# Output projection of the mixer in written order, with the low halves of five activation blocks formed between its blocks

## The chip, the core and the metric

The kernel runs on one core of a Trainium2 chip. A core has five engines with instruction queues of their own: TensorE (PE; its weight loads are shown as PEld), VectorE (DVE), ScalarE (ACT), GpSimd (POOL) and SyncE (SP), which here only issues DMA transfers. The metric is the device time of one execution in microseconds, as the median of several runs. Beside the timed runs stands one execution that the hardware profiler recorded; all rows of a profile are of that execution, and its times are counted from the start of its span.

## The reference, cut to what matters

One layer of a streaming encoder over 512 tokens of 1024 features, in float32:

```python
ada = silu(c) @ w_ada + b_ada
sh1, sc1, g1, sh2, sc2, g2 = split(ada, 6)
h = modulate(rmsnorm(x, norm1_g), sh1, sc1)
z = h @ w_in                                   # five parts of 512 columns
y_a = gate_b * causal_dwconv(gate_c * xa, conv_a_w)
y_b = rg_lru(causal_dwconv(xr, conv_b_w) + conv_b_b, ...) * gelu(gr)
y = concat([head_rmsnorm(y_a), head_rmsnorm(y_b)]) @ w_out     # the output projection
x = x + g1 * y
h = modulate(rmsnorm(x, norm2_g), sh2, sc2)
q = h @ w_q                                    # 8 heads, two halves of 64
# per token and head: the best 16 of 128 keys in each half, the best 16 of their sums,
# softmax g over them, and expert numbers idx
act = gelu(expert_u[idx] . h);  coef = g * act
x = x + g2 * sum(coef * expert_v[idx])
out = rmsnorm(x, final_g)
```

There are 16384 experts. `act` and the sum over `expert_v` are what takes most of the time.

## The kernel before

**Split products.** Most products of float32 matrices are made of three matmuls in a faster type (float32r). A weight block of 1024 x 128 is loaded raw, its high half is the rounded copy that ACT writes (`high`, L74), its low half the difference that DVE writes (`low`, L79); `split_w` does both. `mm3` then issues, for each of the eight slices of 128, high weight by high input (L88), high weight by low input (L89) and low weight by high input (L90). The ring buffers `wraw`, `whi` and `wlo` have four tiles each, and a load into a ring waits until the tile four places earlier has been read.

**Stages, in order.** (1) Norm of x, the first adaLN columns, and the input projection: 20 blocks of `w_in`, between them convolutions, the recurrence and the norm of each head (`head_norm`, L487 to L504), which writes the eight parts of y as halves `ybuf_h` and `ybuf_l`. (2) The output projection: eight blocks of `w_out`, each followed by the residual update of one part of x (`xs`, L618, on DVE) and by the sum of squares (`sq_sum`: square L219 on ACT, addition L221 on DVE). The parts of y are taken in the order 4, 0, 5, 1, 6, 2, 7, 3, in which the head norms deliver them. (3) The second norm: the last update (L628), the mean square of each token (`stat`, L204, and L635), the transposes of x that are stored for the end (`x1_mm`, L588, and `x1_out`, L594, L595), and the modulated h in halves. (4) The query projection, eight blocks of `w_q`, the scores, and the first searches. (5) The activation stage: 124 blocks of 128 experts against 320 tokens that are treated densely; the product with all experts is made on PE, while DVE does the searches, the gate matrices and, for the other 192 tokens' part, dot products with gathered rows of `expert_u`. (6) The value stage: 128 blocks of `expert_v` (and the last four activation blocks), with three matmuls for each product (L1345), while DVE sums gathered rows for 128 tokens (L1083). (7) The final norm.

**Unsplit blocks.** In the activation stage, block 0 is formed in the query stage. Blocks 1 to 11 (`k < FN`, `FN = 12`) are not split: PE multiplies the raw float32 weights by the float32 input `h2f` (L1159), eight matmuls instead of 24. From block 12 on they are split: `w_high(k + 3)` and `w_low(k + 2)` run some blocks ahead. Blocks 5 to 11 are loaded straight into the rings `wlo` and `whi`, which are not needed for halves then.

**The adaLN pieces.** The columns of the second gate (`g2`) come from `ada_gate2`: eight pieces of `w_ada` of 128 x 1024 are loaded on SP (L129), scaled by the conditioning (L159) and added up on DVE (L163, 128 x 1024 each); a pair of matmuls with a column of ones sums over partitions into a row (`row_mm`, L138), ACT copies the row (L143), PE transposes it (four, L146), DVE adds the bias (L150), and the columns are stored to DRAM (`g2d`, L194). Before, this is the last part of the generator `ada_it`, which is stepped between the blocks of the mixer.

**What sets the order.** A planner orders the instructions of each engine by dependences and estimated costs, except inside a `manual_schedule` region: there, each engine issues the region's instructions in the order in which they are written. Where a region's instructions fall among those outside it, and the order across engines, stay with the planner. Before, such a region begins at block 7 of the output projection and ends in the second norm (at part 2 of h); another holds the activation and value stages. In the activation stage the written order itself is made by a small plan: `pe`, `dve` and `ac` add up estimated costs, and for each block DVE is given further work (searches, gates, dot products) as long as `dve[0] < RHO * pe[0]`.

Of the kernel before, what the change touches and what calls it, by code (L numbers as in the profile page):

```python
# [8 lines left out]
F32 = mybir.dt.float32  # L9
# [8 lines left out]
T = 512  # L18
D = 1024
KB = 8  # L20
# [14 lines left out]
def block_kernel(ctx, tc, xT, small, w_ada1, w_ada, b_ada, w_in, w_r, w_i, w_out, w_q, keys, uT, u, v, final_g, out):  # L35
# [46 lines left out]
    def split_w(raw):  # L82
        hi = high(raw)
        return hi, low(raw, hi)
# [47 lines left out]
    def ada_rows():  # L132
        pr = psA.tile([128, T], F32, name="ps_row")
        nc.vector.memset(pr, 0.0)
        return pr
# [19 lines left out]
    def ada_sum(q, every):  # L155
        acc = first.get(q)
        if acc is None:
            acc = piece(0, q, "wacc", 2)
        nc.vector.tensor_scalar(acc, acc, cl[:, 0:1], None, op0=OP.mult)  # L159
        for k in range(1, KB):  # L160
            if k % every == 0:
                yield
            nc.vector.scalar_tensor_tensor(acc, piece(k, q), cl[:, k:k + 1], acc, op0=OP.mult, op1=OP.add)  # L163
        return acc
# [21 lines left out]
        yield  # L186

    def ada_gate2():
        acc = yield from ada_sum(3, 1)
        pr = ada_rows()  # L190
        for b in range(2):
            row_mm(pr, b, ones, acc, True, True)
        ada_cols(pr, 40, 8)
        nc.sync.dma_start(g2d.rearrange("b (m p) -> p (b m)", p=128), adac[:, 40:48])  # L194
        yield
# [258 lines left out]
    def ada_rest():  # L454
        norm2 = ada_norm2()
        for i in range(19):
            if i % 2 == 0:
                next(gate1, None)
            next(norm2, None)
            yield  # L460
        yield from ada_gate2()
    ada_it = ada_rest()


# [129 lines left out]
        nc.scalar.activation(xn, pt, AF.Copy)  # L594
        nc.gpsimd.dma_start(x1d[t * 128:(t + 1) * 128, e * 512:(e + 1) * 512], xn)  # L595

    osp = {}
    qraw, qsp = {}, {}
    for m in range(KB):
        if m + 2 < KB:  # L600
            oraw[m + 2] = load_w(w_out[m + 2])
        else:
            qraw[m + 2 - KB] = load_w(w_q[m + 2 - KB])
        if m < KB - 1:
            osp[m] = split_w(oraw[m])
        if m >= KB - 2:
            for _ in ada_it:
                pass
            osp[KB - 1] = osp.get(KB - 1) or split_w(oraw[KB - 1])
        if m == KB - 1:  # L610
            norm2 = ExitStack()
            norm2.enter_context(tc.manual_schedule())
        hi, lo = osp.pop(m)
        ps = psZ.tile([128, T], F32, name="ps_z", bufs=3)
        mm3(ps, hi, lo, lambda k: ybuf_h[:, k, :], lambda k: ybuf_l[:, k, :], kord, True, True)
        if m == KB - 1:
            break
        nc.vector.scalar_tensor_tensor(xs[:, m, :], ps, adac[:, 16 + m:17 + m], xs[:, m, :], op0=OP.mult, op1=OP.add)  # L618
        sq_sum(m, True)
        next(ada_it, None)  # L620
    mx.close()
    adx.close()
    qp = pro.enter_context(tc.tile_pool(name="qp", bufs=2))
# [476 lines left out]
    def w_load(k):  # L1100
        if k < len(jobs):
            kind, i = jobs[k]
            if 5 <= k < FN:
                raw = wring.tile([128, KB, 128], FR, name=("wlo", "whi")[k % 2], bufs=WB).bitcast(F32)
                nc.sync.dma_start(raw, uT[i])
                wraw[k] = raw
                return
            if k >= K5 and (k - K5) % 5 == 4:
                wraw[k] = gp.tile([128, KB, 128], F32, name="raw5")
                nc.sync.dma_start(wraw[k], uT[i] if kind == "u" else  # L1110
                                  v[vorder[i] * 128:(vorder[i] + 1) * 128, :].rearrange("p (k e) -> p k e", k=KB))
                return
            wraw[k] = load_w(uT[i] if kind == "u" else
                             v[vorder[i] * 128:(vorder[i] + 1) * 128, :].rearrange("p (k e) -> p k e", k=KB))

    def w_high(k):
        if FN <= k < len(jobs):
            whi[k] = high(wraw[k])

    def w_low(k):  # L1120
        if FN <= k < len(jobs):
            wlo[k] = low(wraw.pop(k), whi[k])
            settle()

# [6 lines left out]

    def weights(k):
        w_ahead(k)
        w_low(k + 2)

    act = {0: act0}
# [15 lines left out]
    def u_chunk(k, pool):  # L1152
        c = jobs[k][1]
        if c:
            ps = pool.tile([128, NU], F32, name="ps_act", bufs=3 if pool is psE else 2)
            if k < FN:
                raw = wraw.pop(k)
                for j in range(KB):
                    nc.tensor.matmul(ps, raw[:, j, :], h2f[j // 2][:, j % 2], start=j == 0, stop=j == KB - 1)  # L1159
            else:  # L1160
                mm3(ps, whi.pop(k), wlo.pop(k), hd, ld, range(KB), True, True)
            u_evict()
            unread.append((c, ps))
        q = c // 2 - 2
        if c % 2 == 0 and 0 <= q < v0 // 2:
            spill(q)
        pe[0] += FPE if c and k < FN else 3530
        dve[0] += 0 if c and k < FN - 2 else 1140
        ac[0] += 450 if c and k < FN - 3 else 1400

    gbuf, g16, gdone = {}, {}, set()
    coef = {}
# [95 lines left out]
        w_load(k)  # L1268
    for k in range(1, 3):
        w_high(k)  # L1270
    w_low(1)
    manual = ExitStack()
    manual.enter_context(tc.manual_schedule())
# [169 lines left out]
GS = 32768.0  # L1443
AB = 3
GPE = 460
FN = 12
DX = 0.3
FPE = 4400
SE = 0.65
# [71 lines left out]
```

## Time and profile before

| | us |
|---|---|
| median of 3 runs | 1329.12 (1328.17 to 1332.12) |
| profiled execution | 1328.57 |
| its span, first to last instruction | 1326.8 |
| TensorE busy | 1304.6 (98%) |
| VectorE busy | 1215.5 (92%) |
| ScalarE busy | 728.2 (55%) |
| GpSimd busy | 503.8 (38%) |

In a row of the timeline stand the start, the duration, the engine, the line of the kernel, the operation, what is written and read with the shapes, and in brackets the idle time of the engine just before and what ended it. A group of instructions by line shows the count, then busy time, mean duration in ns, and the idle time before with what ended it. A matmul's record is longer than its distance to the next one, because matmuls overlap; the distance of two starts is what one costs. In this execution the output projection's matmuls run from 159.9 to 207.1 us, the activation stage's unsplit blocks from 279.4 to 326.7, and the value stage's matmuls from 770.9 on.

### The profile page before, as it was taken

Reading aid. Unit: us, or ns where it says so; the run is one execution under the profiler, and the core shown is the slowest. Engines: PE = TensorE matmul, PEld = TensorE weight load, DVE = VectorE, ACT = ScalarE, POOL = GpSimd, SP = SyncE. Lnnn points to the kernel's source line nnn. Section 1 sums busy time; section 2 is a strip of 40 time slices with the busy share of each in tenths; the row PEclk is TensorE's granted clock in tenths of the full one; section 3 lists DMA queues with packets and bytes.
Section 4 is the critical chain, followed back from the end, with each engine's and each line's share of the span. In section 5 each row is a group of like instructions: output and inputs, shape, how many; then the busy total and the mean of one; then the engine's idle time right before and its main releaser. Section 6 shows DMA issues by size and latency. Waiting matters only on the chain.

```text
span 1326.8 us, 21286 instructions
## 1 busy us (share of the span) xinstructions
PE 1304.6 (98%) x7506; PEld 1127.3 (85%) x7506; DVE 1215.5 (92%) x2247; ACT 728.2 (55%) x1319; POOL 503.8 (38%) x336
## 2 busy tenths in 40 slices
PE   8999999999999999999999999999999999999995
PEld 6677777777999999999999998788888888888884
DVE  6889976999999999999999689899899989899998
ACT  4677636424586898878669543334343434343432
POOL 0000001000244121446655356677554656554560
PEclk9999999999999999999999999999999999999998
DMA  9765542163898999999999999999999999999993
GB/s 369 272 242 174 185 133 101 59 210 102 302 355 297 341 326 348 394 366 416 417 413 399 402 358 410 377 408 418 412 415 413 415 412 416 412 415 411 416 401 134
DMA packets 150267, 440.05 MB, mean 332 GB/s; under 512 B 16016, under 2 KB 43664, under 8 KB 150160
## 3 DMA queue, kind: packets, MB, share of 16 engines
q1 hardware_dynamic: 103008, 267.23, 53.9%
q0 software_dynamic: 46864, 170.41, 32.5%
q8 instruction: 59, 0.97, 0.3%
q10 hardware_dynamic: 288, 1.05, 0.2%
q14 instruction: 48, 0.39, 0.1%
HBM read 393.54 MB, written 45.09 MB: 331 GB/s over the span
## 4 chain that ended last, share of the span: by engine, by line
PE 56%; DMA 13%; issue 13%; DVE 12%; POOL 3%; ACT 2%; SPq 1%; DVEq 0%; POOLq 0%; ACTq 0%
DMA wraw<-in_v_dram 10%; PE ps_act L88 10%; PE ps_act L89 9%; PE ps_act L90 9%; PE ps_z L89 4%; PE ps_z L90 4%; PE ps_z L88 4%; PE ps_act L1159 4%; PE ps_gt L908 3%; POOL rows L1045 3%; DVE ys L1083 2%; DVE scr L1066 2%; DVE cl L1236 2%; PE acc L1345 2%; DVE wlo L79 2%
## 5 line engine op out<-in xcount | busy, mean ns | idle before, releaser
L74 ACT ACTIVATE whi<-wraw 128x1024 fp32r<-128x1024 f32 x255 | 269.7, 1058 | 217.6 <-DMA wraw<-in_v_dram 148.3
L79 DVE TENSOR_TENSOR wlo<-wraw,whi 128x1024 fp32r<-128x1024 f32 x255 | 310.5, 1218 | 41.9 <-ACT whi L74 41.4
L88 PE MATMUL ps_act<-h,whi 128*128 128x320 f32 x928 | 291.5, 314 | 0.0
L89 PE MATMUL ps_act<-h,whi 128*128 128x320 f32 x928 | 286.8, 309 | 0.0
L90 PE MATMUL ps_act<-h,wlo 128*128 128x320 f32 x928 | 286.7, 309 | 0.0
L1045 POOL DMA_INDIRECT rows<-in_u_dram,idx_s x128 | 204.8, 1600 | 131.1 <-DVE scr L1066 105.4
L1045 POOL DMA_INDIRECT rows<-in_v_dram,idx_s x128 | 197.0, 1539 | 143.8 <-DVE ys L1083 122.4
L1345 PE MATMUL acc<-whi,cl 128*128 128x512 f32 x744 | 230.0, 390 | 1.6 <-DVE cl L1236 1.4
L1345 PE MATMUL acc<-whi,ch 128*128 128x512 f32 x744 | 229.2, 389 | 0.0
L1345 PE MATMUL acc<-wlo,ch 128*128 128x512 f32 x744 | 229.1, 389 | 0.0
L1045 POOL DMA_INDIRECT rows<-in_u_dram,idx_b x64 | 95.7, 1495 | 237.9 <-DVE scr L1066 179.3
L89 PEld LDWEIGHTS ps_act<-h,whi 128*128 128x128 f32 x928 | 174.4, 188 | 0.2
L88 PEld LDWEIGHTS ps_act<-h,whi 128*128 128x128 f32 x928 | 174.2, 188 | 0.3
L90 PEld LDWEIGHTS ps_act<-h,wlo 128*128 128x128 f32 x928 | 174.2, 188 | 0.0
L1345 PEld LDWEIGHTS acc<-whi,cl 128*128 128x128 f32 x744 | 139.1, 188 | 33.0 <-DVE cl L1236 4.5
L1083 DVE SCALAR_TENSOR_TENSOR ys<-rows,acts,ys 128x1024 f32<-128x1024 f32 x127 | 163.3, 1286 | 1.6
L1345 PEld LDWEIGHTS acc<-wlo,ch 128*128 128x128 f32 x744 | 139.7, 188 | 29.1
L1345 PEld LDWEIGHTS acc<-whi,ch 128*128 128x128 f32 x744 | 139.5, 188 | 28.8
L1066 DVE SCALAR_TENSOR_TENSOR scr<-rows,h2n 128x1024 f16<-128x1024 f32 x128 | 156.2, 1220 | 5.3 <-DMA rows<-in_u_dram,idx_s 3.6
L1150 ACT ACTIVATE act<-ps_act 128x320 f32<-128x320 f32 x127 | 55.9, 440 | 125.6 <-PE ps_act L90 92.8
L896 ACT ACTIVATE igh<-oh,gl 128x128 f16<-128x128 f16 x320 | 99.7, 440 | 0.0
L595 POOL DMA_DIRECT2D x1d<-xn x8 | 4.6, 581 | 214.7 <-ACT xn L594 214.7
(325 smaller groups left out, 1921.6 us busy)
## 6 DMA issues: line engine op xcount, KB each, us to landing
wraw<-in_uT_dram SPq DMA_DIRECT2D x120, 512.0 KB, 7.2
wraw<-in_v_dram SPq DMA_DIRECT2D x103, 512.0 KB, 13.4
Gd<-stg SPq DMA_DIRECT2D x46, 512.0 KB, 8.4
wada<-in_w_ada_dram SPq DMA_DIRECT2D x45, 512.0 KB, 6.1
Ad<-act SPq DMA_DIRECT2D x48, 320.0 KB, 6.6
act<-Ad SPq DMA_DIRECT2D x48, 320.0 KB, 15.0
raw<-in_v_dram SPq DMA_DIRECT2D x25, 512.0 KB, 13.4
h<-Gd SPq DMA_DIRECT2D x12, 1024.0 KB, 18.3
```

Of the source, the lines that this page charges most:

```text
L74: nc.scalar.activation(hi, raw, AF.Copy)
L79: nc.vector.tensor_sub(lo, raw, hi.bitcast(F32))
L88: nc.tensor.matmul(ps, hi[:, k, :], xh(k), start=first and k == ks[0], stop=False)
L89: nc.tensor.matmul(ps, hi[:, k, :], xl(k), start=False, stop=False)
L90: nc.tensor.matmul(ps, lo[:, k, :], xh(k), start=False, stop=last and k == ks[-1])
L896: nc.scalar.activation(ig[:, 1, k // 2, :, k % 2], of[:, k // 2, 0, :, k % 2], AF.Copy, scale=gl[:, t0 + k:t0 + k + 1])
L1045: nc.gpsimd.indirect_dma_start(out=r[:, :], out_offset=None, in_=table, in_offset=bass.IndirectOffsetOnAxis(ap=idxs[:, k:k + 1], axis=0))
L1066: nc.vector.scalar_tensor_tensor(scr, rows.pop(n), 1.0, hn, op0=OP.mult, op1=OP.mult, accum_out=dst[:, k:k + 1])
L1083: nc.vector.scalar_tensor_tensor(ys, rows.pop(k), acts[:, k:k + 1], ys, op0=OP.mult, op1=OP.add)
L1150: nc.scalar.activation(act[c // 2][:, c % 2], ps, AF.Gelu)
L1159: nc.tensor.matmul(ps, raw[:, j, :], h2f[j // 2][:, j % 2], start=j == 0, stop=j == KB - 1)
L1345: nc.tensor.matmul(accs[b][e], st[:, bs], mv[:, e * 512:(e + 1) * 512], start=first, stop=last)
```

## The change

It has three parts.

1. **Order.** The region of written order begins with block 1 of the output projection instead of block 7. In it, the pass of block m issues the loads, block m's matmuls, the residual update of block m - 1, the halves of block m + 1, the square sum of block m - 1, and one step (two in passes 1 and 6) of the second gate's accumulation. The gate's row and its columns are written into pass 7. Halves of blocks 0 and 1 are formed ahead, under the planner, as is block 0 itself.
2. **Low halves ahead.** In passes 1 to 5 the raw weights of activation blocks 1 to 5 (`PM = 5`) are loaded too; in passes 2 to 6 their high and low halves are formed, and the low half is stored to a DRAM tensor `Ld` from GpSimd's queue. In the activation stage, blocks 1 to 5 are split: their raw weights are loaded and the high half is formed again on ScalarE, and the low half is loaded from `Ld` (`low_load`).
3. **Which blocks stay unsplit.** `FN` is 14: blocks 6 to 13 are multiplied unsplit, 10 to 13 of them loaded into the rings `wlo` and `whi`. The estimated costs in the plan follow.

```diff
     def ada_gate2():
-        acc = yield from ada_sum(3, 1)
+        acc = first.pop(3)
+        wts = [None] + [piece(k, 3) for k in (1, 2)]
+        yield
+        nc.vector.tensor_scalar(acc, acc, cl[:, 0:1], None, op0=OP.mult)
+        for k in range(1, KB):
+            yield
+            nc.vector.scalar_tensor_tensor(acc, wts[k], cl[:, k:k + 1], acc, op0=OP.mult, op1=OP.add)
+            if k + 2 < KB:
+                wts.append(piece(k + 2, 3))
         pr = ada_rows()
+        yield
         for b in range(2):
             row_mm(pr, b, ones, acc, True, True)
+        yield
         ada_cols(pr, 40, 8)
...
-        yield from ada_gate2()
     ada_it = ada_rest()
...
-    osp = {}
-    qraw, qsp = {}, {}
+    osp = {m: split_w(oraw[m]) for m in range(2)}
+    qraw, qsp, uraw = {}, {}, {}
+    Ld = dram.tile([PM, 128, D], F32, name="Ld")
+    for _ in ada_it:
+        pass
+    first[3] = piece(0, 3, "wacc", 2)
+    gate2 = ada_gate2()
+    next(gate2)
+
+    def low_ahead(c):
+        raw = uraw.pop(c)
+        lo = low(raw, high(raw))
+        nc.gpsimd.dma_start(Ld[c - 1], lo.bitcast(F32).rearrange("p k e -> p (k e)"))
+
+    psm = {}
+    norm2 = ExitStack()
     for m in range(KB):
+        if m == 1:
+            norm2.enter_context(tc.manual_schedule())
         if m + 2 < KB:
             oraw[m + 2] = load_w(w_out[m + 2])
         else:
             qraw[m + 2 - KB] = load_w(w_q[m + 2 - KB])
-        if m < KB - 1:
-            osp[m] = split_w(oraw[m])
-        if m >= KB - 2:
-            for _ in ada_it:
-                pass
-            osp[KB - 1] = osp.get(KB - 1) or split_w(oraw[KB - 1])
+        if 1 <= m <= PM:
+            uraw[m] = load_w(uT[m])
         if m == KB - 1:
-            norm2 = ExitStack()
-            norm2.enter_context(tc.manual_schedule())
+            next(gate2)
         hi, lo = osp.pop(m)
-        ps = psZ.tile([128, T], F32, name="ps_z", bufs=3)
-        mm3(ps, hi, lo, lambda k: ybuf_h[:, k, :], lambda k: ybuf_l[:, k, :], kord, True, True)
+        psm[m] = psZ.tile([128, T], F32, name="ps_z", bufs=3)
+        mm3(psm[m], hi, lo, lambda k: ybuf_h[:, k, :], lambda k: ybuf_l[:, k, :], kord, True, True)
+        if m == 0:
+            continue
+        p = m - 1
+        nc.vector.scalar_tensor_tensor(xs[:, p, :], psm.pop(p), adac[:, 16 + p:17 + p], xs[:, p, :], op0=OP.mult,
+                                       op1=OP.add)
+        if 2 <= m + 1 < KB:
+            osp[m + 1] = split_w(oraw[m + 1])
         if m == KB - 1:
-            break
-        nc.vector.scalar_tensor_tensor(xs[:, m, :], ps, adac[:, 16 + m:17 + m], xs[:, m, :], op0=OP.mult, op1=OP.add)
-        sq_sum(m, True)
-        next(ada_it, None)
+            next(gate2)
+        sq_sum(p, True)
+        for _ in range({1: 2, 6: 2}.get(m, 1 if m < 6 else 0)):
+            next(gate2)
+        if m - 1 in uraw:
+            low_ahead(m - 1)
...
+    ps = psm.pop(KB - 1)
     mx.close()
     adx.close()
...
-            if 5 <= k < FN:
+            if 4 + PM < k < FN:
...
     def w_high(k):
-        if FN <= k < len(jobs):
+        if k <= PM or FN <= k < len(jobs):
             whi[k] = high(wraw[k])
 
+    def low_load(k):
+        if k <= PM:
+            wlo[k] = wring.tile([128, KB, 128], FR, name="wlo", bufs=WB)
+            nc.sync.dma_start(wlo[k].bitcast(F32).rearrange("p k e -> p (k e)"), Ld[k - 1])
+
     def w_low(k):
-        if FN <= k < len(jobs):
+        if k <= PM:
+            wraw.pop(k)
+        elif FN <= k < len(jobs):
             wlo[k] = low(wraw.pop(k), whi[k])
             settle()
...
     def weights(k):
         w_ahead(k)
+        low_load(k + 3)
         w_low(k + 2)
...
-            if k < FN:
+            if PM < k < FN:
                 raw = wraw.pop(k)
...
-        pe[0] += FPE if c and k < FN else 3530
-        dve[0] += 0 if c and k < FN - 2 else 1140
-        ac[0] += 450 if c and k < FN - 3 else 1400
+        pe[0] += FPE if PM < k < FN else 3530
+        dve[0] += 0 if k < FN - 2 else 1140
+        ac[0] += 450 if PM - 3 < k < FN - 3 else 1400
...
     for k in range(1, 3):
         w_high(k)
+        low_load(k)
...
-FN = 12
+FN = 14
+PM = 5
```

After the loop the written order goes on as before: the halves of the first query block (`qsp[0] = split_w(qraw[0])`), the sum of squares (`stat`), two groups of transposes, the last residual update, and the rest of the norm.

More of the change, by code (lines that the diff above doesn't have):

```diff
@@ L603, in block_kernel @@
             qraw[m + 2 - KB] = load_w(w_q[m + 2 - KB])
-        if m < KB - 1:
-            osp[m] = split_w(oraw[m])
-        if m >= KB - 2:
-            for _ in ada_it:
-                pass
-            osp[KB - 1] = osp.get(KB - 1) or split_w(oraw[KB - 1])
+        if 1 <= m <= PM:
+            uraw[m] = load_w(uT[m])
         if m == KB - 1:
-            norm2 = ExitStack()
-            norm2.enter_context(tc.manual_schedule())
+            next(gate2)
         hi, lo = osp.pop(m)
-        ps = psZ.tile([128, T], F32, name="ps_z", bufs=3)
-        mm3(ps, hi, lo, lambda k: ybuf_h[:, k, :], lambda k: ybuf_l[:, k, :], kord, True, True)
-        if m == KB - 1:
-            break
-        nc.vector.scalar_tensor_tensor(xs[:, m, :], ps, adac[:, 16 + m:17 + m], xs[:, m, :], op0=OP.mult, op1=OP.add)
-        sq_sum(m, True)
-        next(ada_it, None)
+        psm[m] = psZ.tile([128, T], F32, name="ps_z", bufs=3)
[7 more added lines that the diff above has]
+            osp[m + 1] = split_w(oraw[m + 1])
+        if m == KB - 1:
+            next(gate2)
[4 more added lines that the diff above has]
+            low_ahead(m - 1)
+    if KB - 1 in uraw:
+        low_ahead(KB - 1)
+    ps = psm.pop(KB - 1)
     mx.close()
```

## The prediction

> **What bounds the kernel now.** I read the page's busy times first, then busy time by stage, then the timeline of each engine around the output projection, the chain behind it and the start of the activation stage.
>
> ```profile
> PE 1304.6 (98%) x7506; PEld 1127.3 (85%) x7506; DVE 1215.5 (92%) x2247; ACT 728.2 (55%) x1319; POOL 503.8 (38%) x336
> ```
> ```profile
> 160.00:207.00 47.00, 47.00 (x203) 36.57 (x202) 30.86 (x38) 16.80 (x23) 0.00 (x0) 1.00 0.40 126
> 207.00:214.00 7.00, 6.86 (x60) 6.41 (x58) 3.43 (x10) 3.85 (x8) 3.01 (x5) 1.00 0.35 142
> ...
> 327.00:771.00 444.00, 444.00 (x3474) 438.80 (x3473) 415.72 (x803) 342.82 (x785) 178.27 (x116) 1.00 0.97 364
> 771.00:1300.00 529.00, 524.52 (x2338) 434.09 (x2337) 499.45 (x545) 205.95 (x264) 319.20 (x204) 1.00 1.02 407
> ```
>
> The columns are stretch, length, busy PE, PEld, DVE, ACT and POOL, granted clock, DMA share, GB/s. TensorE (PE) sets the pace almost everywhere: 47.00 of 47.00 us in the output projection (160 to 207), 444 of 444 in the activation stage, 524.5 of 529 in the value stage. VectorE (DVE) has room in the projection (30.9 of 47), little later. So each edit is priced by what it does to PE: matmul time removed, or PE made to wait. The one stretch of the change that PE does not pace is 207 to 214: there the norm of the finished sum runs as a chain over all engines.
>
> **The saving: activation blocks.** The eviction of one block follows its last matmul, so the distance of two evictions is the price of a block on PE, unsplit (first pair) and split (second pair):
>
> ```profile
> 314.19 0.44 ACT L1150 ACTIVATE act<-ps_act 128x320 f32<-128x320 f32 x1 [3.01 <-PE ps_act L1159]
> ...
> 318.50 0.44 ACT L1150 ACTIVATE act<-ps_act 128x320 f32<-128x320 f32 x1 [2.92 <-PE ps_act L1159]
> ...
> 330.62 0.44 ACT L1150 ACTIVATE act<-ps_act 128x320 f32<-128x320 f32 x1 [2.12 <-PE ps_act L90]
> 334.14 0.44 ACT L1150 ACTIVATE act<-ps_act 128x320 f32<-128x320 f32 x1 [2.14 <-PE ps_act L90]
> ```
>
> 4.31 us unsplit, 3.52 split: 0.79 apart. Blocks 1 to 5 become split (5 x 0.79 saved), blocks 12 and 13 unsplit (2 x 0.79 spent): **-2.4 us** on PE. It is real only if nothing else is then late. The first low half that DVE makes in this stage is ready long before its use:
>
> ```profile
> 318.27 1.21 DVE L79 TENSOR_TENSOR wlo<-wraw,whi 128x1024 fp32r<-128x1024 f32 x1
> ```
> ```profile
> 327.21 0.31 PE L90 MATMUL ps_act<-h,wlo 128*128 128x320 f32 x1
> ```
>
> That is 7.7 us of cover, and DVE has two lows fewer to form here, so it does not become the bound. The new loads of lows 1 to 5 and the five extra ACT roundings fall where DMA and ACT are mostly idle; with four buffers, low 4 waits for block 0's matmuls and lands some 5 to 7 us later, three blocks (10.6 us) ahead of need: nothing. Bounds: 0 if another engine holds the stage anyway; -4.8 if DVE sets the pace, which loses two lows of 1.21 us beside the -2.4.
>
> **The head of the projection.** Before, the planner runs blocks 0, 1 and 2 side by side while the last head's norm is still on its way, and the gate's eight accumulations (L163) are squeezed between the norm's steps on DVE:
>
> ```profile
> 159.94 0.39 PE L88 MATMUL ps_z<-ybuf_h,whi 128*128 128x512 f32 x1
> ```
> ```profile
> 166.78 0.64 ACT L498 ACTIVATE sq<-mfull 128x512 f32<-128x512 f32 x1
> ```
> ```profile
> 169.03 0.68 DVE L504 TENSOR_TENSOR ybuf_l<-mfull,ybuf_h 128x512 fp32r<-128x512 f32 x1
> 169.63 0.68 DVE L499 SCALAR_TENSOR_TENSOR sq<-ps_rs,sq 128x512 f32<-128x512 f32 x1
> 170.23 1.27 DVE L163 SCALAR_TENSOR_TENSOR wacc<-wada,cl,wacc 128x1024 f32<-128x1024 f32 x1
> 171.43 0.68 DVE L500 SCALAR_TENSOR_TENSOR sq<-sq,mfull 128x512 f32<-128x512 f32 x1
> 172.03 1.28 DVE L163 SCALAR_TENSOR_TENSOR wacc<-wada,cl,wacc 128x1024 f32<-128x1024 f32 x1
> 173.22 0.74 DVE L502 SCALAR_TENSOR_TENSOR mfull<-y,small_sb,sq 128x512 f32<-128x512 f32 x1
> 173.89 1.28 DVE L163 SCALAR_TENSOR_TENSOR wacc<-wada,cl,wacc 128x1024 f32<-128x1024 f32 x1
> 175.08 0.69 DVE L504 TENSOR_TENSOR ybuf_l<-mfull,ybuf_h 128x512 fp32r<-128x512 f32 x1
> ```
>
> The last half of y is there at 175.8; PE was never idle. In the changed kernel the accumulations come after block 0. From L498's end (167.4) the chain is then L499, the other head's L504 and L500 at 0.6 us each, L502 0.67, ACT's rounding about 0.75, L504 0.7: y complete near **171.4**. But the written order lets PE run ahead only in block 1 (block 2 must follow it). Cover from 159.94: 36 matmuls of two blocks at 0.228 us (the step between PE's last two rows below) and three of the norm, to 168.8; six more for the seventh part of y, to 170.2; then idle until the eighth: about **+1.0** (0 if the chain is a microsecond earlier; the upper end is rival B). Block 0 then ends near 172.2.
>
> **The body.** DVE's durations:
>
> ```profile
> L163 DVE SCALAR_TENSOR_TENSOR wacc<-wada,cl,wacc 128x1024 f32<-128x1024 f32 x7 | 8.9, 1277 | 0.0
> L79 DVE TENSOR_TENSOR wlo<-wraw,whi 128x1024 fp32r<-128x1024 f32 x6 | 7.3, 1218 | 0.2
> L618 DVE SCALAR_TENSOR_TENSOR xs<-ps_z,adac,xs 128x512 f32<-128x512 f32 x7 | 5.1, 747 | 10.4 <-PE ps_z L90 10.4
> L221 DVE TENSOR_TENSOR sqa<-sqa,sq 128x512 f32<-128x512 f32 x6 | 4.1, 684 | 0.8 <-ACT sq L219 0.8
> ```
>
> Starts lie some 0.07 us closer than durations. In written order the low half of block 2 stands behind block 0's residual update (L618): 0.7 + 1.2 after block 0's end, while block 1 has only 0.6 us left and two matmuls of block 2 need no low: PE waits about **+1.05** (0 to 2). From then on one pass costs DVE 0.68 + 1.14 + 0.6 + 1.2 + 1.14 (update, next low, square sum, accumulation, low of an activation block) = 4.8 us against 24 x 0.228 = 5.5 on PE, and the next low comes second: hidden. In pass 6 two accumulations and the clearing of the row (0.48) stand before PE's gate row: done about 5.8 us after block 5, PE is there after 5.5: **+0.35** (0 to 1). ACT has 2.7 us a pass. The raw weights: loads go out in order on SP, each held until the low that frees its buffer.
>
> ```profile
> wraw<-in_uT_dram SPq DMA_DIRECT2D x120, 512.0 KB, 7.2
> ...
> wraw<-in_w_out_dram SPq DMA_DIRECT2D x8, 512.0 KB, 3.7
> ...
> x1d<-xn POOLq DMA_DIRECT2D x8, 256.0 KB, 2.4
> ```
>
> The tightest is block 7's: issued after block 5's low, about 15.1 us after block 0's end, landed by 22.3 even at 7.2 us; ACT wants it at 23.4. The five stores on POOL's queue, empty till then, are twice the size of the last row's (estimate 3 to 5 us), and their buffer is taken again two passes (11 us) later. Both cost nothing; a store or load some 6 us longer would show as PE idle in passes 4 to 6.
>
> **The tail.** Before:
>
> ```profile
> 190.43 1.23 DVE L79 TENSOR_TENSOR wlo<-wraw,whi 128x1024 fp32r<-128x1024 f32 x1
> ```
> ```profile
> 196.87 0.60 PE L146 MATMUL ps_row<-ident,wada 128*128 128x128 f32 x4
> ```
> ```profile
> 207.09 0.39 PE L90 MATMUL ps_z<-ybuf_h,wlo 128*128 128x512 f32 x1
> 207.32 0.95 PE L204 MATMUL ps_col<-ones,sqa 128*128 128x1 f32 x8
> ```
> ```profile
> 207.52 0.75 DVE L628 SCALAR_TENSOR_TENSOR xs<-ps_z,adac,xs 128x512 f32<-128x512 f32 x1 [3.24 <-PE ps_z L90]
> 208.30 0.69 DVE L630 TENSOR_TENSOR sq<-xs 128x512 f32<-128x512 f32 x1
> 210.14 0.16 DVE L635 TENSOR_SCALAR rs_m<-ps_col 128x4 f32<-128x4 f32 x1 [1.15 <-PE ps_col L204]
> ```
>
> The first query block's low was made at 190.43 and the gate's transposes at 196.87, in the shade of PE. When PE leaves block 7, DVE starts the last update 0.2 us later. In the changed order the transposes stand behind block 7 on PE, and on DVE in front of that last update: gate column (waits for the transposes, 0.64 after PE's end), square sum 0.6, query low 1.14. The update starts about 2.45 us after block 7 instead of 0.2; part of the old time went to PE's own transposes, so the chain (L635) loses **+2.2** (1.1 to 2.5). PE has only small transposes to do meanwhile. The gate's transposes no longer interrupt the body: **-0.45**.
>
> **The sum**, against the profiled execution (span 1326.8, 1328.57 in all): +1.0 + 1.05 + 0.35 - 0.45 + 2.2 = +4.15 before the query stage, which PE paces, then -2.4 in the activation stage: +1.8, so 1330.4. That execution lies 0.55 below the median shown (1329.12): **1330.9** as a median.
>
> **A rule against it.** PE idles for up to a microsecond at a time around 207 to 214, some 2 us more than now; the granted clock there is 1.00 (row of that stretch). The Trainium skill (TensorE: Matmul & The Clock Gate, What's actually happening) says that the clock halves after an idle window of about 3.4 us. By the trace no idle comes near that, and the sum stays; it enters as rival E.
>
> **Rivals.**
> - B, slower: the planner puts block 1 behind all of block 0. Nothing in the row of 159.94 forbids it; the three blocks side by side speak against it. PE then loses the cover of 18 matmuls, 18 x 0.228 = 4.1 us: 1335.0. It decides if block 1's first matmul starts after block 0's last.
> - C: the saving of 2.4 us stops short of the end, because the value stage waits for transfers (DMA share 1.02 there). Against it: 524.5 of 529 us busy PE. 1333.3.
> - D: the 4.15 us are absorbed, by a head without idling and PE work filling the tail. For it: 32 transposes lie there; against it: they are in a fixed order. -2.4: 1326.7.
> - E: clock loss. The last 27 us of the kernel have a clock of 0.82; that over the 17 us after 214 would be 17 x 0.22 = 3.7 more: 1334.6.
>
> ```profile
> 1300.00:1327.00 27.00, 15.85 (x64) 12.56 (x63) 20.97 (x43) 6.27 (x20) 0.00 (x0) 0.82 0.26 98
> ```
> - F, faster: DVE's two lows fewer also remove the value stage's 4.5 us of PE idle (529 less 524.5), with D: 1322.2.
>
> That the change does not do what it says (low halves not in time, PE waiting at blocks 1 to 5) is part of the left-over.
>
> **How the numbers follow.** Forecast 0.60, B 0.12, C 0.08, D 0.11, E 0.03, F 0.04, left-over 0.02. 0.3% is 4.0 us, about what a measurement of this kernel can tell from no change: same is 1325.1 to 1333.1. The forecast's own range by its bounds is 1327 to 1333.5. Faster: F and the low ends of D, 0.10. Slower: B, E, half of C and the forecast's high end, 0.23. Same 0.67. Range: from below D to just above B, 1325.5 to 1336.
>
> **What would show it.** Right: unsplit blocks 8 instead of 11 at 4.31 us; blocks 1 and 2 of the activations 3.52 apart; block 2's third projection matmul waiting for a low; the last residual update about 2.4 us after block 7's last matmul, behind the gate column and the query low; the first split block of 14 on some 1.8 us later than now's block 14. Wrong: PE idle of over 2 us before y is complete (B), the last update directly after block 7 (D), PE waits for lows read back from DRAM, or a value stage of other length by more than 3 us.

## The result and the profile after

The changed kernel takes **1344.65 us** (median of 6 runs, 1343.72 to 1351.48) where the kernel before takes 1329.90 beside it: a ratio of **1.0119** (95% interval 1.0105 to 1.0132). The forecast was 1330.9, at most 1336. The profiled execution has a span of 1342.0 us against 1326.8, so 15.2 us are to be found.

The head of the page of the kernel after: busy time with share of the span, and the granted clock in 40 slices of 33.5 us.

```profile
PE 1306.6 (97%) x7530; PEld 1129.8 (84%) x7530; DVE 1219.6 (91%) x2250; ACT 736.1 (55%) x1327; POOL 512.1 (38%) x341
...
PEclk9999997999999999999999999999999999999999
```

PE's busy time has hardly grown (1304.6 to 1306.6), so the time is in waiting, and the seventh slice (201 to 235 us) has a clock digit of 7 (70 to 80%), where the kernel before has 9 (90% or more) in every slice but its last. That points at the end of the output projection. Marks of the kernel after, from its timeline (first and last matmul of the projection, the mean square, the first query copy, the evictions of activation blocks 1, 2 and 5, the first matmul of the value stage):

```profile
159.72 0.40 PE L88 MATMUL ps_z<-ybuf_h,whi 128*128 128x512 f32 x1
...
213.05 0.39 PE L90 MATMUL ps_z<-ybuf_h,wlo 128*128 128x512 f32 x1
...
218.35 0.16 DVE L667 TENSOR_SCALAR rs_m<-ps_col 128x4 f32<-128x4 f32 x1 [1.15 <-PE ps_col L214]
...
249.22 0.60 ACT L760 ACTIVATE qT<-ps_z 128x512 f32<-128x512 f32 x1 [0.41 <-PE ps_z L90]
...
300.61 0.44 ACT L1190 ACTIVATE act<-ps_act 128x320 f32<-128x320 f32 x1 [1.17 <-PE ps_act L90]
304.13 0.44 ACT L1190 ACTIVATE act<-ps_act 128x320 f32<-128x320 f32 x1 [2.13 <-PE ps_act L90]
...
314.69 0.44 ACT L1190 ACTIVATE act<-ps_act 128x320 f32<-128x320 f32 x1 [3.08 <-PE ps_act L90]
...
787.14 0.63 PE L1386 MATMUL acc<-whi,ch 128*128 128x512 f32 x2
```

The same marks before and after, and how far the kernel after is behind:

| mark | before | after | behind |
|---|---|---|---|
| first matmul of the projection | 159.94 | 159.72 | -0.2 |
| last one | 207.09 | 213.05 | +6.0 |
| mean square (L635, now L667) | 210.14 | 218.35 | +8.2 |
| first query copy | 231.87 | 249.22 | +17.4 |
| eviction of activation block 1 | 284.05 | 300.61 | +16.6 |
| of block 5 | 301.27 | 314.69 | +13.4 |
| of block 13 | 334.14 | 349.15 | +15.0 |
| first matmul of the value stage | 770.85 | 787.14 | +16.3 |
| its last | 1315.46 | 1330.31 | +14.9 |

So the tail and the activation blocks go about as forecast, and the head costs less (the terms are below). Two losses stand beside them that the forecast did not have: 6 us inside the projection, and 9 us between the mean square and the first query copy.

**The first loss.** The issue of the first low half's store, and the waits of DVE and PE, in the projection after (in brackets, the idle time before the instruction and what ended it):

```profile
179.31 0.73 POOL L618 DMA_DIRECT2D Ld<-wlo  x1 [178.03 <-DVE wlo L79]
```
```profile
182.50 1.22 DVE L79 TENSOR_TENSOR wlo<-wraw,whi 128x1024 fp32r<-128x1024 f32 x1
183.63 0.75 DVE L639 SCALAR_TENSOR_TENSOR xs<-ps_z,adac,xs 128x512 f32<-128x512 f32 x1
188.05 1.23 DVE L79 TENSOR_TENSOR wlo<-wraw,whi 128x1024 fp32r<-128x1024 f32 x1 [3.67 <-DMA Ld<-wlo]
...
199.19 1.22 DVE L79 TENSOR_TENSOR wlo<-wraw,whi 128x1024 fp32r<-128x1024 f32 x1 [1.59 <-DMA Ld<-wlo]
...
203.64 0.48 DVE L134 MEMSET ps_row<- 128x512 f32 x1
```
```profile
204.28 1.87 PE L138 MATMUL ps_row<-wacc,ones 128*1 128x512 f32 x4 [4.18 <-DVE ps_row L134]
206.08 0.80 PE L88 MATMUL ps_z<-ybuf_h,whi 128*128 128x512 f32 x1
206.67 0.63 PE L89 MATMUL ps_z<-ybuf_l,whi 128*128 128x512 f32 x1
207.10 0.63 PE L90 MATMUL ps_z<-ybuf_h,wlo 128*128 128x512 f32 x1
207.53 0.63 PE L88 MATMUL ps_z<-ybuf_h,whi 128*128 128x512 f32 x1
```

DVE wants to form a low half of a `w_out` block and waits 3.67 us, later 1.59, until a store of an activation block's low half has landed: the ring tile that it is to fill is still being stored. All that stands behind it on DVE is late, up to the clearing of the gate's row, and PE waits 4.2 us for that. After the wait the matmuls start 0.43 us apart instead of 0.228, until 209.6.

**The second loss.** ACT copies x out of the accumulators into a ring of four tiles, which POOL stores (`x1d`). The waits on ACT, and the stores' issues on POOL, after:

```profile
218.84 1.09 ACT L603 ACTIVATE xn<-ps_g 128x512 f32<-128x512 f32 x2
228.46 0.60 ACT L603 ACTIVATE xn<-ps_z 128x512 f32<-128x512 f32 x1 [8.53 <-DMA x1d<-xn]
```
```profile
217.21 1.08 POOL L604 DMA_DIRECT2D x1d<-xn  x2 [11.14 <-ACT xn L603]
219.73 1.07 POOL L604 DMA_DIRECT2D x1d<-xn  x2 [1.44 <-ACT xn L603]
```

The fifth copy waits 8.5 us for the first store. Before, such a store landed 2.4 us after its issue; here the first takes some 11 us. Stretches of the kernel after (length, busy PE, PEld, DVE, ACT, POOL, granted clock, DMA share, GB/s):

```profile
217.00:219.00 2.00, 1.74 (x16) 1.75 (x17) 0.55 (x4) 0.77 (x3) 1.08 (x2) 1.00 0.38 4
219.00:221.00 2.00, 2.00 (x21) 2.00 (x20) 0.77 (x4) 0.93 (x2) 1.07 (x2) 1.00 1.08 47
221.00:223.00 2.00, 1.55 (x14) 0.98 (x11) 0.84 (x2) 0.00 (x0) 0.00 (x0) 1.00 0.37 23
223.00:225.00 2.00, 0.00 (x0) 0.00 (x0) 0.00 (x0) 0.00 (x0) 0.00 (x0) 1.00 0.35 20
225.00:227.00 2.00, 0.00 (x0) 0.00 (x0) 0.00 (x0) 0.00 (x0) 0.00 (x0) 0.90 0.64 193
227.00:229.00 2.00, 0.00 (x0) 0.00 (x0) 0.00 (x0) 0.54 (x2) 0.00 (x0) 0.50 1.02 414
```

From 217 to 225 the DMA engines are 35 to 108% busy and move 4 to 47 GB/s; only then does the rate jump to 193 and 414. Something with much time and few bytes is in front. What is new there is the store of the second gate, 4 KB in 1024 elements of 4 bytes. The first two lines are its issue in the kernel before, and its size and its time from issue to landing there; the third is its issue in the kernel after:

```profile
197.70 0.38 SPq L194 DMA_DIRECT2D g2d<-adac  x1
```
```profile
g2d<-adac SPq DMA_DIRECT2D x1, 4.0 KB, 8.9
```
```profile
214.11 0.38 SPq L204 DMA_DIRECT2D g2d<-adac  x1
```

Before, it went out long ahead of x1 and took 8.9 us where nothing waited for it; after, it is issued 3.1 us before the first store of x1. PE has nothing from 222.7 to 229.8 us, and its clock falls to 0.50.

### The profile page after: what moved, and what is told of

Same layout as the page of the kernel before. It is cut to its first block, busy times and chain, and to the rows that moved or that the text cites. A ratio compares the mean times of both kernels' runs of the same rounds, so it can differ in the third digit from the quotient of the medians.

```text
span 1342.0 us, 21379 instructions
## 1 busy us (share of the span) xinstructions
PE 1306.6 (97%) x7530; PEld 1129.8 (84%) x7530; DVE 1219.6 (91%) x2250; ACT 736.1 (55%) x1327; POOL 512.1 (38%) x341
## 3 DMA queue, kind: packets, MB, share of 16 engines
q1 hardware_dynamic: 104448, 272.47, 54.7%
q10 hardware_dynamic: 288, 1.05, 0.2%
## 4 chain that ended last, share of the span: by engine, by line
PE 55%; DMA 15%; DVE 14%; issue 12%; SPq 2%; ACT 1%; POOL 1%; DVEq 0%; ACTq 0%; POOLq 0%
PE ps_act L88 9%; PE ps_act L89 9%; PE ps_act L90 9%; DMA wraw<-in_v_dram 7%; PE acc L1386 6%; PE ps_z L89 4%; PE ps_z L88 4%; PE ps_z L90 4%; DVE ys L1115 3%; PE ps_gt L940 3%; PE ps_act L1199 3%; DMA rows<-in_u_dram,idx_s 2%; DVE cl L1276 2%; DVE scr L1098 2%; DVE wlo L79 2%
## 5 line engine op out<-in xcount | busy, mean ns | idle before, releaser
L74 ACT ACTIVATE whi<-wraw 128x1024 fp32r<-128x1024 f32 x263 | 277.7, 1058 | 213.0 <-DMA wraw<-in_v_dram 126.5
L79 DVE TENSOR_TENSOR wlo<-wraw,whi 128x1024 fp32r<-128x1024 f32 x258 | 314.4, 1219 | 49.2 <-ACT whi L74 43.5
L88 PE MATMUL ps_act<-h,whi 128*128 128x320 f32 x952 | 299.0, 314 | 0.0
L89 PE MATMUL ps_act<-h,whi 128*128 128x320 f32 x952 | 294.2, 309 | 0.0
L90 PE MATMUL ps_act<-h,wlo 128*128 128x320 f32 x952 | 294.1, 309 | 0.0
L1386 PE MATMUL acc<-whi,cl 128*128 128x512 f32 x744 | 229.8, 390 | 3.3 <-DVE cl L1276 3.2
L88 PEld LDWEIGHTS ps_act<-h,whi 128*128 128x128 f32 x952 | 178.7, 188 | 0.7
L89 PEld LDWEIGHTS ps_act<-h,whi 128*128 128x128 f32 x952 | 178.9, 188 | 0.2
L90 PEld LDWEIGHTS ps_act<-h,wlo 128*128 128x128 f32 x952 | 178.7, 188 | 0.0
L1190 ACT ACTIVATE act<-ps_act 128x320 f32<-128x320 f32 x127 | 55.8, 439 | 116.1 <-PE ps_act L90 89.5
L1269 ACT ACTIVATE ch<-cf 128x768 fp32r<-128x768 f32 x64 | 54.2, 847 | 68.2 <-DVE cf L1262 38.7
```

Of the source, the lines that this page charges most:

```text
L74: nc.scalar.activation(hi, raw, AF.Copy)
L79: nc.vector.tensor_sub(lo, raw, hi.bitcast(F32))
L88: nc.tensor.matmul(ps, hi[:, k, :], xh(k), start=first and k == ks[0], stop=False)
L89: nc.tensor.matmul(ps, hi[:, k, :], xl(k), start=False, stop=False)
L90: nc.tensor.matmul(ps, lo[:, k, :], xh(k), start=False, stop=last and k == ks[-1])
L1190: nc.scalar.activation(act[c // 2][:, c % 2], ps, AF.Gelu)
```

## Experiments on the second loss: the gate's store

**Its place alone.** The changed kernel with the store issued in the activation stage:

```diff
-        nc.sync.dma_start(g2d.rearrange("b (m p) -> p (b m)", p=128), adac[:, 40:48])
...
     for k in range(CE):
+        if k == 4:
+            nc.sync.dma_start(g2d.rearrange("b (m p) -> p (b m)", p=128), adac[:, 40:48])
         weights(k)
```

> The changed kernel with one instruction moved: the store of the second gate (1024 elements of 4 bytes) is issued in the activation stage, at block 4, instead of right before the second norm. Theory 1 (this store's tiny packets hold up the w_q load and the stores of x1 behind it, so ScalarE's fifth copy waits for a buffer): that wait falls from 8.5 us to under 1 us, the first qT copy from 249.2 to about 240 us, its clock dip goes, and the time is 1334 to 1336 us. Rival (the stores of the low halves or the w_q load hold up the stores of x1, whatever the gate's store does): the wait stays above 5 us and the time at 1342 to 1346 us.

1334.68 us, ratio 1.0028 (1.0013 to 1.0042); the first query copy at 238.98. ACT's fifth copy:

```profile
219.12 0.60 ACT L602 ACTIVATE xn<-ps_z 128x512 f32<-128x512 f32 x1 [0.30 <-DMA x1d<-xn]
```

One instruction was worth 10 us. From the mean square to the first query copy this kernel takes 21.7 us, the kernel after 30.9. Up to the mean square it stays late (217.24, after: 218.35), so the two losses are separate. The 1.1 us between these two marks come before the store is issued: PE waits as long for the gate's row (4.1 us), but the half clock behind that wait ends at about 208.3 us instead of 209.5 (granted clock from 205 to 210 us 0.67 instead of 0.55).

**The other way round, a miss.** The kernel before with the store placed later in the program:

```diff
-        nc.sync.dma_start(g2d.rearrange("b (m p) -> p (b m)", p=128), adac[:, 40:48])
...
     stat(sqs[0], True, False)
+    nc.sync.dma_start(g2d.rearrange("b (m p) -> p (b m)", p=128), adac[:, 40:48])
```

> The kernel before with the same one instruction moved the other way: the store of the second gate right after the first half of the sum of squares, where the changed kernel has it; everything else as before. Theory 1: the wait of ScalarE's copies for the stores of x1 grows from 0.6 us to 7 us or more and the time is 1336 to 1340 us. Rival (the store alone is harmless, and only with the other transfers of the change is it slow): 1328 to 1332 us.

1330.80 us, ratio 1.0005 (0.9991 to 1.0018), which would be the rival. But the edit had moved nothing in time:

```profile
198.16 0.38 SPq L625 DMA_DIRECT2D g2d<-adac  x1
```

SP had nothing to do and the gate was ready, so the store went out at 198.16, as good as before (197.70). The run says nothing on either theory. To make a store late, what it reads has to be late:

```diff
-        nc.sync.dma_start(g2d.rearrange("b (m p) -> p (b m)", p=128), adac[:, 40:48])
...
+    g2c = const.tile([128, 8], F32, name="g2c")
+    nc.vector.tensor_copy(g2c, adac[:, 40:48])
+    nc.sync.dma_start(g2d.rearrange("b (m p) -> p (b m)", p=128), g2c)
     sq = sq_pool.tile([128, T], F32, name="sq")
     nc.vector.tensor_mul(sq, xs[:, m, :], xs[:, m, :])
```

> The kernel before, with the store of the second gate really made late: it reads a copy of the gate that VectorE makes (8 columns, some 0.1 us) after the last update of the residual, so it is issued at about 208.5 us instead of 197.7, just ahead of the stores of x1 (first at 209.7). No other part of the change is in it. Theory 1 (the tiny packets of this store hold up what is queued behind it): ScalarE's fifth copy of x1 waits until about 216 to 218 us instead of 212.3, the first qT copy comes 4 to 8 us later, time 1334 to 1339 us. Rival (the hold-up needs the w_q load or the stores of lows beside it): 1329 to 1332 us, fifth copy before 213.5 us.

1355.89 us, ratio 1.0181 (1.0164 to 1.0198): more than either theory allowed. The hold-up was there (8.63 us on ACT, first query copy +10.5), but the value stage was also 19 us longer (first to last accumulating matmul 563.9 us against 544.6). Two runs told the parts apart: the same with the copy in a dead tile (one whose content nothing reads any more), so that no tile changes its address (`g2c = l4[:, 0:2]`), and the kernel before with nothing but the 32-byte tile and the copy.

> As the kernel before with the gate's store delayed to about 208.5 us, but the copy that it reads lies in 8 columns of a tile that is dead by then (l4), so that no tile lies at another address than before. That run was 24 us slower: 10.5 us up to the first qT copy (the hold-up of x1's stores) and some 19 us more in the value stage, at 395 to 400 GB/s instead of 413 to 415. Theory 5 (the 19 us come from the 32-byte tile, which moves every tile allocated after it): the hold-up stays, the value stage is as long as before, time 1339 to 1343 us. Rival (they come from the lateness itself, through the order of the transfers): 1352 us or more.

> The kernel before with the 32-byte tile and VectorE's copy into it alone; the gate's store is where it was. Theory 5: the transfers of the value stage run at 395 to 405 GB/s and the time is 1341 to 1350 us, with no wait for x1's stores over 1 us. Rival: 1329 to 1333 us.

The first: 1340.74 us, ratio 1.0089 (1.0070 to 1.0107), value stage 544.3 us, and on ACT and SP:

```profile
220.22 0.60 ACT L593 ACTIVATE xn<-ps_z 128x512 f32<-128x512 f32 x1 [8.68 <-DMA x1d<-xn]
```
```profile
208.20 0.38 SPq L630 DMA_DIRECT2D g2d<-l  x1
```

So this store alone, with no low halves, no `w_q` load beside it and no written order, holds x1's stores up for 8.7 us, and it costs the kernel before 10 us. The second: 1347.82 us, ratio 1.0129 (1.0113 to 1.0146), ACT's wait 0.61 us, and in the value stage (first two rows; the other two are the kernel before)

```profile
1000.00:1100.00 100.00, 99.63 (x440) 82.19 (x439) 94.51 (x88) 36.86 (x47) 57.81 (x39) 1.00 1.04 398
1100.00:1200.00 100.00, 97.49 (x427) 79.39 (x426) 87.56 (x82) 37.95 (x49) 55.01 (x35) 1.00 1.03 400
```
```profile
1000.00:1100.00 100.00, 99.95 (x441) 82.26 (x440) 93.08 (x87) 37.07 (x47) 56.92 (x38) 1.00 1.04 413
1100.00:1200.00 100.00, 100.00 (x443) 82.73 (x442) 95.26 (x89) 41.22 (x52) 59.70 (x38) 1.00 1.03 415
```

398 to 400 GB/s at the same DMA share, where the kernel before has 413 to 415 (1000 to 1200 us). A tile that nothing reads costs 17 us, in a stage whose DMA share is 1.03. It moves the tiles that are allocated after it by 32 bytes; that this is the cause fits both runs, but which tiles' addresses matter was not tried. How the lower rate reaches PE is not shown either: the wait that grows there is put down to DVE's coefficients (10.6 us instead of 1.4 on the busiest line).

**Elements or bytes.** The changed kernel, store in its place, the same 4 KB in 128 elements of 32 bytes:

```diff
-        nc.sync.dma_start(g2d.rearrange("b (m p) -> p (b m)", p=128), adac[:, 40:48])
+        nc.sync.dma_start(g2d.rearrange("b f -> (b f)").rearrange("(p m) -> p m", m=8), adac[:, 40:48])
```

> The changed kernel with the gate's store at the same place and of the same 4 KB, but as 128 elements of 32 bytes instead of 1024 of 4 (the gate's columns then stand in another order in DRAM, so the final gating uses permuted columns; nothing else is touched). Theory 1, as told by the number of elements: the wait of ScalarE's fifth copy falls from 8.5 us to under 2 us, time 1334 to 1337 us. Rival (any store at this place holds the others up, whatever its elements): wait over 6 us, 1343 us or more.

1334.47 us, ratio 1.0039 (1.0019 to 1.0059), and

```profile
219.10 0.60 ACT L603 ACTIVATE xn<-ps_z 128x512 f32<-128x512 f32 x1 [0.25 <-DMA x1d<-xn]
```

With an eighth of the elements the hold-up is gone; it lies in how the 4 KB are cut up, not in the place or the bytes. The edit changes the number of elements, their size and their order in DRAM together, so which of these counts is not told apart. The Trainium skill (DMA: Bandwidth & Descriptors, Rules for kernel authors) says that a last dimension that is not contiguous becomes one descriptor for each element. The packets agree: the queue that carries SP's transfers has 104448 of them in the kernel after and 103552 here, 896 fewer, which is 1024 less 128. The same page (Issuing engines are not separate DMA queues) says that transfers issued by SP and POOL run on the same 16 engines. That agrees too: a store issued on SP held up four issued on POOL, by 8.5 us.

## Experiments on the first loss: the tiles of the low halves

**Tiles of their own**, in memory that the mixer's blocks have left free:

```diff
+    mixx.close()
...
+    lap = la.enter_context(tc.tile_pool(name="lap", bufs=2))
...
-        lo = low(raw, high(raw))
+        hi = high(raw)
+        lo = lap.tile([128, KB, 128], FR, name="wla", bufs=2)
+        nc.vector.tensor_sub(lo, raw, hi.bitcast(F32))
```

> The changed kernel with two buffers of their own for the low halves that are formed ahead, in memory that the mixer's blocks have left free, so that no split of a w_out block waits for their stores. Theory 2 (VectorE waits 3.7 and 1.6 us for these stores, is late with the gate's sum, TensorE idles 4.4 us before the gate's row, and the clock is halved after that): the wait before the row falls under 1 us, the spacing of the matmuls behind it stays at 0.23 us, w_out ends 5 to 7 us earlier, time 1337 to 1340 us. Rival (VectorE is late by the sum of its work alone, or the clock falls whatever the wait does): less than 3 us saved, 1341.5 us or more.

1339.49 us, ratio 1.0070 (1.0052 to 1.0089). PE at the gate's row:

```profile
199.96 1.03 PE L138 MATMUL ps_row<-wacc,ones 128*1 128x512 f32 x4 [0.61 <-DVE ps_row L134]
200.92 0.50 PE L88 MATMUL ps_z<-ybuf_h,whi 128*128 128x512 f32 x1
201.25 0.40 PE L89 MATMUL ps_z<-ybuf_l,whi 128*128 128x512 f32 x1
```

The wait is 0.61 instead of 4.18 us, the matmuls behind it are 0.23 us apart, and the projection ends at 206.28, 6.8 us earlier.

**Wait or clock.** The changed kernel with matmuls that nothing reads in place of the idling, to tell what the idling itself costs:

```diff
         if m == KB - 1:
+            idle = psA.tile([128, T], F32, name="ps_rs")
+            for i in range(18):
+                nc.tensor.matmul(idle, bdh[:, i % KB, :], ybuf_h[:, i % KB, :], start=True, stop=True)
             next(gate2)
```

> The changed kernel with 18 matmuls of no use (about 4.1 us) in front of the gate's row, where TensorE idles 4.4 us for VectorE; nothing reads them. Theory 4 (the idle stretch itself halves the clock afterwards, 1.0 to 0.5 for some 5 us): the wait stays, filled, the spacing of the matmuls behind it stays at 0.23 us instead of 0.43, w_out ends 2 to 3 us earlier and the time is 1341 to 1343 us. Rival (the clock falls for the load on the chip, or by time): spacing still above 0.35 us, time 1344 us or more.

1341.95 us, ratio 1.0074 (1.0056 to 1.0092). The fill and what follows it on PE:

```profile
198.93 4.24 PE L634 MATMUL ps_rs<-ybuf_h,bdh 128*128 128x512 f32 x18
203.18 1.03 PE L138 MATMUL ps_row<-wacc,ones 128*1 128x512 f32 x4
204.14 0.50 PE L88 MATMUL ps_z<-ybuf_h,whi 128*128 128x512 f32 x1
204.48 0.40 PE L89 MATMUL ps_z<-ybuf_l,whi 128*128 128x512 f32 x1
204.72 0.40 PE L90 MATMUL ps_z<-ybuf_h,wlo 128*128 128x512 f32 x1
```

PE was held as long, but the clock stayed at 1.00 and the spacing at 0.23 us. From the row's first matmul to the projection's last, the kernel after takes 8.8 us (204.28 to 213.05), this one 6.4 (203.18 to 209.53): 2.4 us were the price of the clock after the idle. That price is not fixed: in the two runs that change only the gate's store, the same wait of 4.1 us was followed by 3.4 us of half clock instead of 6.8, and the same stretch took 7.9 us. The median is 2.7 us below that of the kernel after, at the middle of what theory 4 gave; by ratios to the kernel before beside each, the distance is 6 us, more than that theory accounts for.

**The order alone**, without low halves made ahead (`FN = 12`, `PM = 0`, gate's store in the activation stage):

> The written order alone: no low halves formed ahead, none in DRAM, blocks 1 to 11 unsplit as before; the gate's store in the activation stage. Theory 2 (only the stores' hold on the buffers makes VectorE late): the gate's row waits under 1 us, the clock stays at 1.0, w_out ends at 206 to 208 us, and with the tail's 2.2 the time is before +2 to +4, 1332.5 to 1334.5 us. Rival (the order by itself makes VectorE late): the row waits 3 us or more, clock 0.5, time 1336 us or more.

1332.05 us, ratio 1.0004 (0.9994 to 1.0014), a little under what was expected.

```profile
199.52 1.03 PE L138 MATMUL ps_row<-wacc,ones 128*1 128x512 f32 x4 [0.34 <-DVE ps_row L134]
```

The row waits 0.34 us, the projection runs from 159.50 to 205.82 (46.3 us; before 47.15), the mean square follows 5.30 us after its last matmul instead of 3.05. So the order does not make DVE late; the stores did.

## Experiments on what is left

**Both repairs**: tiles of their own and the gate's store in the activation stage.

> Both edits at once. If theories 1 and 2 hold and are independent, the savings add: 1344.6 less 9 to 10 less 5 to 7, that is 1328 to 1331 us, level with the kernel before; what is then left of the written order (the tail +2.2 us, the low of block 2 about +0.6, the head) is paid for by the four blocks that are split again at 0.785 us each less. If the two stalls cover each other, 1333 us or more.

1331.80 us, ratio 1.0005 (0.9989 to 1.0021), 0.8 us above the range expected. Counted from the projection's first matmul, the value stage begins after 627.4 us in the kernel after, 617.2 with the store moved, 619.6 with the tiles, 610.8 with both (before: 610.9): 10.2 and 7.8 alone, 16.6 together. Of the 10.2, 1.2 fall in the projection, where the half clock happened to be shorter; without them the two add up (9.0 and 7.8).

**The tail of before** on top of that: square sum and query split ahead of the last update, the gate's columns behind it.

```diff
-        if m == KB - 1:
-            next(gate2)
         sq_sum(p, True)
+        if m == KB - 1:
+            qsp[0] = split_w(qraw[0])
...
     stat(sq, False, True)
+    next(gate2)
```

> The kernel with both earlier edits (gate's store in the activation stage, low halves in buffers of their own), and the tail's order of before again: the square sum and the split of the first query block ahead of the last update, the gate's columns behind it. Theory 3 (these steps on VectorE in front of the last update cost 2.2 us of the chain to the mean): the mean is formed about 3.1 us after the last matmul of w_out instead of 5.3, first qT copy near 232.5, time 1328.5 to 1330.5 us. Rival (TensorE's waits in the query stage take the gain back): 1331 to 1332.5 us.

**1328.05 us, ratio 0.9975** (0.9963 to 0.9986): faster than the kernel before by a quarter of a percent. DVE and PE at the end of its projection:

```profile
205.88 0.39 PE L90 MATMUL ps_z<-ybuf_h,wlo 128*128 128x512 f32 x1
```
```profile
206.31 0.75 DVE L665 SCALAR_TENSOR_TENSOR xs<-ps_z,adac,xs 128x512 f32<-128x512 f32 x1 [2.28 <-PE ps_z L90]
207.09 0.69 DVE L667 TENSOR_TENSOR sq<-xs 128x512 f32<-128x512 f32 x1
209.42 0.17 DVE L150 TENSOR_TENSOR adac<-ps_row,small_sb 128x8 f32<-128x8 f32 x1 [1.64 <-PE ps_row L146]
209.51 0.15 DVE L674 TENSOR_SCALAR rs_m<-ps_col 128x4 f32<-128x4 f32 x1
```

The mean square comes 3.6 us after the last matmul instead of 5.3; the last half microsecond was not won, because the gate's columns now stand in front of it. How much of the gain belongs to the change is open: the value stage begins 1.0 us earlier than before, counted from the projection's first matmul (609.9 against 610.9), and the rest is a value stage that is 2.4 us shorter (542.2 against 544.6), a length that differs from kernel to kernel as the next run shows.

**Blocks 12 and 13 split again** (`FN = 12`) in that kernel:

> The kernel with both repairs and the tail of before, and blocks 12 and 13 split again (unsplit: 6 to 11 instead of 6 to 13). By the distance of evictions, 2 x 0.79 us less on TensorE: 1325.5 to 1328 us, or 0.997 to 0.996 of before. Rival (VectorE, with two lows of 1.2 us more to form in the activation stage, or the value stage's transfers take it back): as the kernel with FN = 14, 0.9975 or more.

1332.88 us, ratio 1.0015 (1.0006 to 1.0023): slower, against the expectation. The two blocks did save: from the first query copy to the value stage 536.4 us against 538.3. But the value stage (first to last accumulating matmul) took 550.1 us against 542.2. In the kernels here without the 32-byte tile that stage lasts 542 to 550 us (before 544.6). Why it is long in this one was not found; the order of transfers and DVE's steps is planned anew for each kernel, and PE's waits for coefficients doubled (2.3 to 5.1 us on one line, 1.5 to 2.9 on another), which is not all of 8 us.

## Why the prediction was wrong, point by point

- **Bound and method** (PE sets the pace; price by what PE loses): right. All of the loss is PE waiting, and the clock behind it.
- **Head +1.0, rival B**: blocks 0 and 1 ran side by side and PE never idled; y was complete at 169.6 instead of 171.4. Measured 0, the lower bound given.
- **Low half of block 2, +1.05**: PE's step there is 0.75 us instead of 0.228, with and without the repairs: about +0.5. The figures beside the term give 0.7 + 1.2 - 0.6 - 2 x 0.228 = 0.84, so 0.2 of the 1.05 had no row behind it.
- **Gate's row, +0.35**: 0.34 us of wait in the order alone, 4.18 in the changed kernel. This is the first failed step, and its root is the sentence that the five stores cost nothing, because they take "3 to 5 us" and "their buffer is taken again two passes (11 us) later". Both numbers were wrong. The first low half was formed at 177.8 to 179.0 and stored at 179.3; DVE wanted its tile for another at 184.4, 5.4 us after it was formed, and got it at 188.05, 8.7 us after the store's issue. The ring did not go round by places: the fourth tile, with block 3's low half, had been read by 183.1, and yet the wait is for the tile of the first activation low half. That fits a ring that gives out the tile which the program released first, since this one's only reader, the store, is written right behind it. The store was estimated from a smaller one on quiet queues (2.4 us); in the projection the DMA share was 0.27 before (173 to 207 us) and 0.79 after (173 to 213). The warning that "a store or load some 6 us longer would show as PE idle in passes 4 to 6" named the place, with the idling right behind them.
- **Tail +2.2**: 5.30 us from last matmul to mean square against 3.05, +2.25: right, and undone by its reversal as far as 0.6.
- **The moved store of the gate**: never priced. The columns were moved behind block 7, and the sum counted their work on PE and DVE, not the transfer that ends them, although the trace of before had it: issued at 197.70, landed at 206.64, 8.9 us for 4 KB. Moved in front of the stores of x1 it costs 9 to 10 us. This is the second failed step and the larger one: a step that moves takes its DMAs along.
- **Activation blocks -2.4**: from the first query copy to the eviction of block 13, 102.27 us before and 99.93 after: -2.3. Right in size. At the end of that stage 1.1 are left (538.98 to 537.92).
- **Rival E, clock loss** (chance 0.03): it came, twice, but as a consequence of waits that the sum held to be absent. The row of the kernel after for 205 to 210 us (the columns as above):

```profile
205.00:210.00 5.00, 5.00 (x14) 3.15 (x11) 0.90 (x2) 2.06 (x3) 0.53 (x1) 0.55 0.70 200
```

The clock is 0.55 after the idle of 4.2 us, and 0.50 from about 227 to 237 us, in and after the idle of 7.1 us that begins at 222.7. The rule of the Trainium skill that the prediction weighed (TensorE: Matmul & The Clock Gate, What's actually happening: half clock after an idle window of about 3.4 us) agrees with both, and with the fill, after which it stayed at 1.00. But the traces do not bear it out as a limit: in the kernel before, PE idled 2.87 us up to 1299.56, and its matmuls then came 0.43 us apart until 1302.7; an idle of 2.2 us at 984 us was followed by half clock in the run with the store moved (0.57 from 986 to 990 us) and not in the run with the store packed (1.00). The prediction's error was to hold that no idle would come near the limit.
- **Range**: no rival priced a transfer that holds up others, so the upper end of 1336 only held the written order's own costs.

The sum as it should have stood, from the projection's first matmul to the first query copy (89.5 us after, 71.9 before), stretch by stretch and with the run of the order alone as the measure between: 1.4 us for the order (2.25 for the tail, less 0.8 that the projection became shorter), 7.0 for the stores' hold on the tiles (a projection of 53.3 us instead of 46.3; 2.4 of it clock), and 9.1 for the gate's store (30.9 us from the mean square to the first query copy instead of 21.7). That is 17.5, and 17.6 were measured. Each of the two losses also goes with its own edit alone: the projection takes 46.6 us with the tiles, the later stretch 21.7 with the store moved. The activation blocks give 1.1 back by the value stage, which lasts 1.4 us less than before.

## What to carry to other kernels

When an instruction is moved, follow what hangs on its result to the end, its store included, and ask what that store will now stand in front of; 4 KB in 4-byte elements took 8.9 us, where the median load of 512 KB took 3.7 us for `w_out` and 7.2 for the activation stage's weights. A tile that leaves through a store is busy until the store has landed, so a ring shared with short-lived tiles runs at the speed of the slowest store: give it tiles of its own, or count the landing time, not the issue. And PE's idling of 4 us and more was paid twice here, since matmuls behind it ran at half the clock.

## What the runs showed of the hardware that was not expected

- A store of 1024 elements of 4 bytes held back four 256 KB stores from another engine's queue by 8.5 us; in 128 elements of 32 bytes the same wait was 0.25 us.
- A store placed later in the program of an idle SP went out at the same time (198.16 against 197.70): on that queue, place is not time.
- 32 bytes of tile memory that nothing used lowered the transfer rate of the value stage from 413 to 415 GB/s to 398 to 400 and cost 17 us (ratio 1.0129). The same copy into a tile that was there already had no such effect (value stage 544.3 us).
- After an idle of 4.1 to 4.2 us, PE ran at half clock for 6.8 us in one kernel and for 3.4 in two others with the same wait.
